# Six modulation buffers in two sets of three, with layer 1's gate tiles in one set and asked for over three groups

## The chip, the core and the metric

The kernel runs on one NeuronCore of one Trainium2 chip. The metric is the device time of one execution in microseconds (us). "PE" is TensorE, "DVE" VectorE, "ACT" ScalarE, "POOL" GpSimd and "SP" SyncE; SP and POOL issue the DMAs, and each issues its own in the order of its list.

## The reference

Two layers of a hybrid encoder over 512 positions of width 2048, in float32. For each layer:

```
mod = silu(c) @ w_ada + b_ada            # 2048 -> 3 x 2048
shift, scale, gate = split(mod)
h = layernorm(x) * (1 + scale) + shift
u_f, z_f, cq, ckv, k_r, z_a = split(h @ w_in)     # 1024 1024 512 256 64 1024
y_f = real(fft over positions and channels of u_f) @ w_fmix * silu(z_f)
q   = rmsnorm(cq) @ w_q_b ;  kv = rmsnorm(ckv) @ w_kv_b ;  rotary on q and k_r
y_a = attention(q, k, v) * silu(z_a)              # 8 heads, not causal
x   = layernorm(alpha * x + gate * (concat(y_f, y_a) @ w_out)) * ln_g + ln_b
```

## The kernel before

**Numbers in two halves.** Each float32 operand is split into a rounded half `hi` and a remainder `lo` (`split`: an ACT cast at L148, a DVE subtraction at L149), and each product is three matmuls (`mm3`, L152 to L154). A weight tile is loaded by SP into one of three raw buffers (pool `wrp`), cast on ACT and subtracted on DVE; the raw buffer is free again after the subtraction.

**Order.** The kernel is written with tile pools. A scheduler lays the program out into one list for each engine and puts in the semaphore waits; each engine then works strictly through its list. A tile of a pool waits for the last reader of the tile that had its buffer before.

**The modulation, L206 to L283.** The product with `w_ada` is not done on PE: tiles of `w_ada` of 128 x 1024 (512 KB) are loaded (`ada_load`), and one DVE instruction a tile multiplies it by a column of silu(c) and adds it to a sum (L246 the first of a block, L248 the rest). A block of 1024 output columns takes 16 tiles; then PE transposes the sum (L261), DVE adds it up (L262). The gate of a layer is two blocks, called block 1 and block 2 below: 32 tiles. Layer 1's gate tiles are loaded by POOL (L213, the `GP` branch); all other modulation tiles by SP. A block's steps stand in a generator; `bg_step(n)` adds n to a credit and takes one step for each whole unit of it, so that n is the number of tiles asked for at one unit of the main program.

**Where the tiles live.** The pool `adp` has six buffers of 4 KB a partition under one tag. They hold, one after another, modulation tiles, the scratch `junk` of a normalisation, transposed x (`xT`), in layer 1 six of the folded Fourier constants (`fc`, L567), and at the end the rows of ln_g and ln_b (`lgb`, L1312, four tiles a layer). While the Fourier stage of layer 1 needs the six constants, no gate tile can be loaded.

**Layer 1's first half.** The in-projection comes in groups of columns: U and ZF[0], then the folded Fourier transform of U (`u_pass`, `fourier_folded`; its last steps L863 to L865 run beside the group ZF[1]), then CQ, CKV and ZA[1]. A group is eight units: one weight tile each, multiplied into four PSUM banks of the pool `psa`, which has four banks. So a group can begin in a bank only when the group before is read out of it: ZF[1] by `unfolded` (ACT copy L880, DVE L881 and L882, ACT silu L883, stored to `szd` by SP), CQ by `latent` (ACT copy L916 of two banks, DVE L917 and L918, then squares on ACT, the power on POOL at L190, the scaling on DVE at L927; PE then transposes the result at L933). Beside CQ, `gates` loads the stored silu values back and multiplies the Fourier rows by them on DVE (L873). Gate tiles are asked for at 0.8 a unit in ZF[0] (`G0`), at 1.6 a unit in CKV and ZA[1] (`G1`), and what is left at 1.4 a unit in the output projection (`CP`). The lines are:

```
banks = fm_group(ada=G0)
...
lq = latent_q(tm_group(CQ, runner(gt)))
...
lkv = latent_kv(tm_group(CKV, runner(lq), G1))
...
unfolded(fm_group(last, G1), 4)
```

**The end.** The output projection takes four groups of eight units; after the first, the gate row of layer 1 must be there: the second block's sum (L261, L262), a store of the gate to DRAM (L270) and its load, spread over the partitions (L1284, L1299), and then the first product with it on DVE (L1257).

Of the kernel before, what the change touches and what calls it, by code (L numbers as in the profile page):

```python
# [9 lines left out]
F32 = mybir.dt.float32  # L10
# [8 lines left out]
P = 128  # L19
S = 512  # L20
# [62 lines left out]
def trunk_kernel(ctx: ExitStack, tc: tile.TileContext, x, c, positions, w_ada, b_ada, w_in, q_norm,  # L83
# [4 lines left out]
    SZ = [1, 2, 3, 4, 6]  # L88
    LEADS = [0.5, 0.6, 0.7, 0.5, 0.5]

    ZP, ZL, AP, CP, G0, G1 = 0.5, 1.0, 1.0, 1.4, 0.8, 1.6

    DL0, DLY = 2, 3

# [15 lines left out]
    wrp = ctx.enter_context(tc.tile_pool(name="wrp", bufs=3))  # L110
    acp = ctx.enter_context(tc.tile_pool(name="acp", bufs=2))
    bp = ctx.enter_context(tc.tile_pool(name="bp", bufs=35))
    adp = ctx.enter_context(tc.tile_pool(name="adp", bufs=6))
    t2p = ctx.enter_context(tc.tile_pool(name="t2p", bufs=9))
    smp = ctx.enter_context(tc.tile_pool(name="smp", bufs=4))
    psa = ctx.enter_context(tc.tile_pool(name="psa", bufs=4, space=PSUM))
# [5 lines left out]
    def nm(s):  # L122
        uid[0] += 1
        return f"{s}{uid[0]}"

    def big(shape, dt=F32R):
        return bp.tile(shape, dt, tag="b", name=nm("b"))
# [3 lines left out]

    def t2(shape, dt=F32):
        return t2p.tile(shape, dt, tag="t2", name=nm("t2"))

    def sm(n, tag):
        return smp.tile([P, n], F32, tag=tag, name=nm(tag), bufs=4 if tag in ('mx', 'ssum') else 2)
# [4 lines left out]
    def pm():  # L141
        return psm.tile([P, 512], F32, tag="pm", name=nm("pm"))

    def f(ap):
        return ap.bitcast(F32)
# [22 lines left out]
    for tb in range(NT):  # L168
        t = [big([P, 1024], F32) for _ in range(2)]
# [17 lines left out]
    def rsqrt_eps(dst, src, n, tag, mul=1.0):  # L187
        t = sm(n, tag + "_v")
        V.tensor_scalar(t, src, mul, EPS, op0=ALU.mult, op1=ALU.add)
        GP.tensor_tensor(dst, t, mhalf[:, :n], op=ALU.pow)  # L190
# [15 lines left out]
    def ada_load(l, r, nr, pieces):  # L206
        w, o = sum(n for _, n in pieces), 0
        if l == 0 and pieces[0][0] < SZ[0] * P:
            t = big([P, nr, w], F32)
        else:  # L210
            t = adp.tile([P, nr, w], F32, tag="ada", name=nm("ada"))
        for c0, n in pieces:
            (GP if l == 1 and c0 >= 32 * P else SP).dma_start(t[:, :, o:o + n],  # L213
                         w_ada[l].rearrange("(p r) c -> p r c", p=P)[:, r:r + nr, c0:c0 + n])
            o += n
        return t
# [104 lines left out]
    def ln_stats(stats, tag):  # L321
        mv = sm(2, tag + "_mv")
        V.bn_aggr(mv, stats)
        rstd = sm(1, tag + "_rstd")
        rsqrt_eps(rstd, mv[:, 1:2], 1, tag)
        return mv, rstd

    def bns():
        return smp.tile([P, 4, 6], F32, tag="bns", name=nm("bns"))
# [7 lines left out]
    def normalise(t, sums=None, note=None):  # L337

        nmr, nmean = sm(1, 'nmr'), sm(1, 'nmean')
        if sums is not None:  # L340
            acc, rstd = sm(2, 'lnacc'), sm(1, 'ln_rstd')
            def junk():
                return adp.tile([P, 1024], F32, tag="ada", name=nm("junk"))

            V.tensor_scalar(nmean, sums[:, 0:1], sums[:, 1:2], -1.0 / D, op0=ALU.add, op1=ALU.mult)
            for j in range(2):
                A.activation(junk(), t[j], AF.Square, bias=nmean, accum_out=acc[:, j:j + 1])
            var = sm(1, 'var')
            V.tensor_scalar(var, acc[:, 0:1], acc[:, 1:2], None, op0=ALU.add)
            rsqrt_eps(rstd, var, 1, 'ln', 1.0 / D)  # L350
        else:
            stats = bns()
            for j in range(4):
                V.bn_stats(stats[:, j], t[j // 2][:, (j % 2) * 512:(j % 2) * 512 + 512])
            mv, rstd = ln_stats(stats, 'ln')
            V.tensor_scalar(nmean, mv[:, 0:1], -1.0, None, op0=ALU.mult)
        V.tensor_tensor(nmr, nmean, rstd, op=ALU.mult)
        if note is not None:
            note.extend([sums[:, 1:2], acc[:, 0:1], rstd])
        for j in range(2):  # L360
            A.activation(t[j], t[j], AF.Identity, scale=rstd, bias=nmr)
# [3 lines left out]
    def transposed(xh, k):  # L365
        ps = pm()
        for tb in range(NT):
            PE.transpose(out=ps[:, tb * P:(tb + 1) * P],
                         in_=xh[tb][k // 8][:, (k % 8) * P:(k % 8) * P + P], identity=ident)
        return ps  # L370
# [79 lines left out]
    def scaled(hi, lo, src, g):  # L450
        A.activation(hi, src, AF.Copy, scale=g)
        V.scalar_tensor_tensor(out=lo, in0=src, scalar=g, in1=f(hi), op0=ALU.mult, op1=ALU.subtract)
# [31 lines left out]
    CQ, CKV, UA, UB = (CQ0, 512), (CKV0, 320), (U0, 512), (U0 + 512, 512)  # L484
# [76 lines left out]
    def folded_constants(l):  # L561


        def keep(shape, dt=F32R):
            n[0] += 1
            if n[0] <= 6:
                return adp.tile(shape, dt, tag="ada", name=nm("fc"))  # L567
            return big(shape, dt)

        n = [0]  # L570
        cw, nq, dt = [[None, None], [None, None]], [], []
        cc = big([P, 2, P], F32)
        GP.dma_start(cc, chan.rearrange("a p c -> p a c"))
        wf = big([P, G, P], F32)
        SP.dma_start(wf, w_fmix[l].rearrange("g m d -> m g d"))
        for hf in range(2):
            for a in range(3):
                lhs = big([P, P], F32)
                if a < 2:
                    for d in range(2):  # L580
                        V.tensor_copy(lhs[:, d * 64:d * 64 + 64], cc[:, a, 0:64])
                else:
                    V.tensor_copy(lhs, cc[:, 0, 64:65].broadcast_to([P, P]))
                ps = pm()
                PE.matmul(ps, lhs, wf[:, hf * 4:hf * 4 + 4].rearrange("p g d -> p (g d)"), start=True, stop=True)
                t = keep([P, 2, 512])
                if a < 2:
                    GP.memset(f(t), 0.0)
                    for d in range(2):
                        rs = slice(d * 64, d * 64 + 64)  # L590
                        o, i = (x.rearrange("p (g e c) -> p g e c", e=2, c=P)[:, :, d] for x in (t[rs, 0], ps[rs]))
                        A.copy(o, i)
                        V.tensor_tensor(t[rs, 1].rearrange("p (g e c) -> p g e c", e=2, c=P)[:, :, d], i, f(o),
                                        op=ALU.subtract)
                    cw[a][hf] = t
                else:
                    for g in range(4):
                        cs, m = slice(g * P, g * P + P), ident[:, 120 + hf * 4 + g:121 + hf * 4 + g]
                        scaled(t[:, 0, cs], t[:, 1, cs], ps[:, cs], m)
                    nq.append(t)  # L600
        for k in range(2):
            t = keep([P, 2, S])
            for a in range(2):
                GP.dma_start(t[:, a], dft[a, k * P:(k + 1) * P, :])
            dt.append(t)
        return cw, nq, dt
# [21 lines left out]
    xT = []  # L628

    def make_xT(k0, k1):  # L630
        for k in range(k0, k1, 2):
            if k0 == 0:
                t = adp.tile([P, 2, S], F32, tag="ada", name=nm("xT"))
            else:
                t = big([P, 2, S], F32)
            for i in range(2):
                A.copy(t[:, i], transposed(xt, k + i))
            xT.append(t)
# [47 lines left out]
    for l in range(DEPTH):  # L686
        sums = {}

        def tm_group(g, work=lambda: None, ada=0):
            banks = [pa() for _ in range(NT)]  # L690
            for k2 in range(8):
                tm_half(banks, st.next(), h, k2 * 2, g[1], k2 == 0, k2 == 7)
                bg_step(ada)
                if k2 < 7:
                    work()
            return banks
# [189 lines left out]
        def runner(gen, n=1):  # L886
            def run():
                for _ in range(n):
                    next(gen, None)
            return run  # L890
# [79 lines left out]
        def latent_q(src):  # L970
            p = latent(src, 512, 512)
            yield
            cq.extend(to_feat(p, k) for k in range(4))
# [146 lines left out]
        if l == 0:  # L1120

            for step, (k0, nk) in enumerate(STEPS):
# [5 lines left out]
                if final:  # L1128
                    cw, dt = fourier_weights(0)
# [50 lines left out]
                lq = latent_q(pq)  # L1180
# [20 lines left out]
        else:  # L1201
# [5 lines left out]
            cw, nq, dt = folded_constants(1)  # L1207
# [2 lines left out]
            unfolded(fm_group(runner(fb, FW)), H + 4)  # L1210
            drain(fb)
            gt = gates()
            lq = latent_q(tm_group(CQ, runner(gt)))
            drain(gt)
            next(lq)
            lkv = latent_kv(tm_group(CKV, runner(lq), G1))
# [14 lines left out]
        for i in range(len(todo) + WL):  # L1231
# [9 lines left out]
            if i < 4:  # L1241
                for k in range(2 * i, 2 * i + 2):
                    t = big([P, 2, S])
# [9 lines left out]
        lgb = {}  # L1253
# [26 lines left out]
        for g in range(4):  # L1280
# [21 lines left out]
            else:  # L1302
# [6 lines left out]
                    tm_half(banks, st.next(), y, k2 * 2, 512, k2 == 0, False)  # L1309
                ws = [st.next() for _ in range(KO, 8)]  # L1310
                for i, src in enumerate((ln_g, ln_b)):
                    lgb[i] = [adp.tile([P, 1024], F32, tag='ada', name=nm('lgb')) for _ in range(2)]  # L1312
                    for j in range(2):
                        SP.dma_start(lgb[i][j], src[l:l + 1, j * 1024:(j + 1) * 1024].broadcast_to([P, 1024]))
                if l == 0:
# [79 lines left out]
```

## Time and profile before

| | us |
|---|---|
| median of 3 runs | 1399.76 (1399.33 to 1401.72) |
| profiled execution | 1403.96 |
| its span | 1402.2 |
| PE busy in the span | 1344.2 (96%) |
| DVE busy | 1013.9 (72%) |
| ACT busy | 582.3 (42%) |
| POOL busy | 55.4 (4%) |

Times inside the kernel are counted from the start of the span, on the profiled execution. Rows of the trace are read so: start, duration, engine, line, operation, output and input tiles by the program's names, and in square brackets the time that the engine sat idle before and what released it. "x3" stands for three instructions one behind the other. A DMA's row on POOL or SP is its issue; its landing is told apart. In layer 1 the group ZF[1] ends and CQ begins near 955, CKV begins near 1003, and the first group of the output projection ends near 1255.

### The profile page before, as it was taken

The page shows a single profiled execution, that of the slowest core. Times are in us where ns is not written, and L with a number is a line of the kernel's source. Part 1 is how long each engine was busy: PE and PEld are TensorE (multiplying, and loading weights), DVE is VectorE, ACT ScalarE, POOL GpSimd, SP SyncE. Part 2 cuts the span into 40 slices and gives each one's busy share as a digit, 9 for nine tenths or more (in the row PEclk, how much of TensorE's full clock was granted, in tenths as well). Part 3 has the DMA queues.
Part 4 walks back from the last instruction along what each step waited for, and adds up shares of the span by engine and source line. Part 5 has one row for each costly group of instructions (what it writes and reads, how often), then busy time and mean ns, then how long its engine had stood idle before and what let it go on. Part 6 is the DMA issues. An engine that isn't in the chain of part 4 may idle for free.

```text
span 1402.2 us, 18752 instructions
## 1 busy us (share of the span) xinstructions
PE 1344.2 (96%) x6979; PEld 1139.3 (81%) x6979; DVE 1013.9 (72%) x1667; ACT 582.3 (42%) x1057; POOL 55.4 (4%) x82
## 2 busy tenths in 40 slices
PE   3899999999999999999998999999999999999996
PEld 3688888787888888878877888887898888888885
DVE  7899999948978986659588658557655576642448
ACT  5713323224537777212248524323234677721210
POOL 1000000000000000000022001011000000000001
PEclk9999999999999999999999999999999999999998
DMA  9988898923763542967446345369544221263323
GB/s 269 290 297 273 276 328 287 361 78 98 224 209 101 181 157 87 326 232 269 138 149 226 107 123 166 105 210 359 170 119 121 74 67 53 83 233 105 91 60 120
DMA packets 134547, 253.26 MB, mean 181 GB/s; under 512 B 19308, under 2 KB 50168, under 8 KB 134456
## 3 DMA queue, kind: packets, MB, share of 16 engines
q1 hardware_dynamic: 127416, 228.73, 50.2%
q0 software_dynamic: 7040, 23.34, 4.8%
q8 instruction: 55, 0.90, 0.3%
q14 instruction: 36, 0.29, 0.1%
HBM read 237.32 MB, written 14.70 MB: 180 GB/s over the span
## 4 chain that ended last, share of the span: by engine, by line
PE 80%; DMA 7%; DVE 7%; issue 3%; ACT 2%; POOL 1%; SPq 0%; DVEq 0%; ACTq 0%; POOLq 0%
PE pa L154 18%; PE pa L152 18%; PE pa L153 18%; PE pm L152 6%; PE pm L153 6%; PE pm L154 6%; DMA ada<-in_w_ada_dram 4%; DMA wr<-in_w_in_dram 3%; PE pm L1091 2%; DVE b L149 2%; PE pa L1071 1%; PE pa L1072 1%; DVE acc L248 1%; ACT b L148 1%; PE pm L261 1%
## 5 line engine op out<-in xcount | busy, mean ns | idle before, releaser
L152 PE MATMUL pa<-b,b 128*128 128x512 f32 (+4 forms) x1408 | 526.9, 376 | 12.3 <-ACT b L148 5.8
L153 PE MATMUL pa<-b,b 128*128 128x512 f32 (+4 forms) x1408 | 525.7, 374 | 1.0 <-DVE b L149 0.9
L154 PE MATMUL pa<-b,b 128*128 128x512 f32 (+4 forms) x1408 | 525.0, 374 | 1.0 <-DVE b L149 1.0
L148 ACT CAST b<-wr 128x1024 fp32r<-128x1024 f32 (+3 forms) x182 | 177.9, 988 | 360.0 <-PE pa L154 181.2
L152 PEld LDWEIGHTS pa<-b,b 128*128 128x128 f32 x1408 | 264.6, 189 | 59.9 <-ACT b L148 9.4
L149 DVE TENSOR_TENSOR b<-wr,b 128x1024 fp32r<-128x1024 f32 (+3 forms) x182 | 205.6, 1140 | 136.3 <-PE pa L153 84.5
L154 PEld LDWEIGHTS pa<-b,b 128*128 128x128 f32 x1408 | 265.5, 189 | 47.3 <-DVE b L149 2.1
L153 PEld LDWEIGHTS pa<-b,b 128*128 128x128 f32 x1408 | 265.7, 189 | 44.7 <-DVE b L149 1.9
L248 DVE SCALAR_TENSOR_TENSOR acc<-ada,cact,acc 128x1024 f32<-128x1024 f32 (+2 forms) x193 | 227.4, 1184 | 22.6 <-DMA ada<-in_w_ada_dram 20.6
L152 PE MATMUL pm<-b,b 128*128 128x512 f32 (+3 forms) x594 | 201.5, 341 | 2.1 <-DVE b L1155 0.9
L153 PE MATMUL pm<-b,b 128*128 128x512 f32 (+3 forms) x594 | 197.0, 333 | 0.0
L154 PE MATMUL pm<-b,b 128*128 128x512 f32 (+3 forms) x594 | 196.7, 332 | 0.0
L152 PEld LDWEIGHTS pm<-b,b 128*128 128x128 f32 x594 | 111.6, 188 | 19.3 <-ACT b L148 2.7
L153 PEld LDWEIGHTS pm<-b,b 128*128 128x128 f32 x594 | 112.1, 189 | 10.5
L154 PEld LDWEIGHTS pm<-b,b 128*128 128x128 f32 x594 | 112.1, 189 | 10.6
L148 ACT CAST b<-pm 128x512 fp32r<-128x512 f32 (+4 forms) x110 | 55.0, 531 | 72.6 <-PE pm L835 17.8
L149 DVE TENSOR_TENSOR b<-pm,b 128x512 fp32r<-128x512 f32 (+4 forms) x110 | 64.2, 610 | 24.1 <-ACT b L148 23.5
L1155 DVE TENSOR_TENSOR b<-b,pm 128x512 f32<-128x512 f32 (+1 forms) x88 | 55.2, 656 | 5.2 <-PE pm L154 5.0
L148 ACT CAST b<-t 128x512 fp32r<-128x512 f32 (+1 forms) x73 | 36.0, 526 | 30.8 <-PE pm L153 9.6
L1074 DVE TENSOR_REDUCE mx<-pa 128x1 f32<-128x512 f32 x64 | 42.9, 684 | 5.2 <-PE pa L1072 4.7
L1079 ACT ACTIVATE t<-t,ssum 128x512 f32<-128x512 f32 x64 | 45.9, 736 | 1.1 <-DVE ssum L1078 1.1
L1077 ACT ACTIVATE t<-pa,mx 128x512 f32<-128x512 f32 x64 | 44.0, 694 | 4.6 <-DVE mx L1074 4.5
(208 smaller groups left out, 1175.3 us busy)
## 6 DMA issues: line engine op xcount, KB each, us to landing
wr<-in_w_in_dram SPq DMA_DIRECT2D x105, 512.0 KB, 4.6
ada<-in_w_ada_dram SPq DMA_DIRECT2D x96, 512.0 KB, 5.4
wr<-in_w_out_dram SPq DMA_DIRECT2D x64, 512.0 KB, 4.2
ada<-in_w_ada_dram SPq DMA_DIRECT2D x96, 256.0 KB, 4.9
ada<-in_w_ada_dram POOLq DMA_DIRECT2D x32, 512.0 KB, 5.5
b<-in_x_dram SPq DMA_DIRECT2D x16, 512.0 KB, 6.8
ada<-in_w_ada_dram SPq DMA_DIRECT2D x32, 192.0 KB, 4.7
wr<-in_w_q_b_dram SPq DMA_DIRECT2D x48, 128.0 KB, 3.0
```

The costliest lines, as they stand in the source:

```text
L148: A.copy(hi, src)
L149: V.tensor_tensor(lo, src, f(hi), op=ALU.subtract)
L152: PE.matmul(o, lh, rh, start=first, stop=False)
L153: PE.matmul(o, lh, rl, start=False, stop=False)
L154: PE.matmul(o, ll, rh, start=False, stop=last)
L248: V.scalar_tensor_tensor(out=a, in0=t[:, r - r0], scalar=cact[:, r:r + 1], in1=a, op0=ALU.mult, op1=ALU.add)
L261: PE.transpose(out=ps[:, o:o + P], in_=acc[:, a, (i + j) * P:(i + j + 1) * P], identity=ident)
L1074: V.reduce_max(mx, ps, axis=AX.X, negate=True)
L1077: A.activation(e, ps, AF.Exp, bias=mx, accum_out=ssum)
L1079: A.activation(e, e, AF.Copy, scale=ssum)
L1091: PE.transpose(out=ps[:, o:o + P], in_=es[q2][:, kb * P:(kb + 1) * P], identity=ident)
L1155: V.tensor_tensor(s_[tb], s_[tb], banks[tb][:, :n], op=ALU.add)
```

## The change

The pool gets two tags, `ada` and `adb`, of three buffers each, through a helper `ad`. It deals tiles out in turn to the two tags, except layer 1's gate tiles (`first`): those always take `ada` and do not count as a turn. The junk, constants, xT and lgb tiles go through `ad` too. The six buffers together are as large as before. `G1` goes from 1.6 to 1.0, and the group CQ is given `G1` too, so that after ZF[0] gate tiles are asked for at one a unit in CQ, CKV and ZA[1]. That makes 6 + 24 tiles, and the last two are asked for in the output projection; before it was 6 + 26. Lines from 141 on stand seven lines further down.

```diff
--- before.py
+++ after.py
@@ -88,7 +88,7 @@
     SZ = [1, 2, 3, 4, 6]
     LEADS = [0.5, 0.6, 0.7, 0.5, 0.5]
 
-    ZP, ZL, AP, CP, G0, G1 = 0.5, 1.0, 1.0, 1.4, 0.8, 1.6
+    ZP, ZL, AP, CP, G0, G1 = 0.5, 1.0, 1.0, 1.4, 0.8, 1.0
 
     DL0, DLY = 2, 3
 
@@ -110,7 +110,7 @@
     wrp = ctx.enter_context(tc.tile_pool(name="wrp", bufs=3))
     acp = ctx.enter_context(tc.tile_pool(name="acp", bufs=2))
     bp = ctx.enter_context(tc.tile_pool(name="bp", bufs=35))
-    adp = ctx.enter_context(tc.tile_pool(name="adp", bufs=6))
+    adp = ctx.enter_context(tc.tile_pool(name="adp", bufs=3))
     t2p = ctx.enter_context(tc.tile_pool(name="t2p", bufs=9))
     smp = ctx.enter_context(tc.tile_pool(name="smp", bufs=4))
     psa = ctx.enter_context(tc.tile_pool(name="psa", bufs=4, space=PSUM))
@@ -131,6 +131,13 @@
 
     def t2(shape, dt=F32):
         return t2p.tile(shape, dt, tag="t2", name=nm("t2"))
+
+    turn = [0]
+
+    def ad(shape, dt, s, first=False):
+
+        turn[0] += 0 if first else 1
+        return adp.tile(shape, dt, tag="ada" if first or turn[0] % 2 else "adb", name=nm(s))
 
     def sm(n, tag):
         return smp.tile([P, n], F32, tag=tag, name=nm(tag), bufs=4 if tag in ('mx', 'ssum') else 2)
@@ -208,7 +215,7 @@
         if l == 0 and pieces[0][0] < SZ[0] * P:
             t = big([P, nr, w], F32)
         else:
-            t = adp.tile([P, nr, w], F32, tag="ada", name=nm("ada"))
+            t = ad([P, nr, w], F32, "ada", l == 1 and pieces[0][0] >= 32 * P)
         for c0, n in pieces:
             (GP if l == 1 and c0 >= 32 * P else SP).dma_start(t[:, :, o:o + n],
                          w_ada[l].rearrange("(p r) c -> p r c", p=P)[:, r:r + nr, c0:c0 + n])
@@ -340,7 +347,7 @@
         if sums is not None:
             acc, rstd = sm(2, 'lnacc'), sm(1, 'ln_rstd')
             def junk():
-                return adp.tile([P, 1024], F32, tag="ada", name=nm("junk"))
+                return ad([P, 1024], F32, "junk")
 
             V.tensor_scalar(nmean, sums[:, 0:1], sums[:, 1:2], -1.0 / D, op0=ALU.add, op1=ALU.mult)
             for j in range(2):
@@ -564,7 +571,7 @@
         def keep(shape, dt=F32R):
             n[0] += 1
             if n[0] <= 6:
-                return adp.tile(shape, dt, tag="ada", name=nm("fc"))
+                return ad(shape, dt, "fc")
             return big(shape, dt)
 
         n = [0]
@@ -630,7 +637,7 @@
     def make_xT(k0, k1):
         for k in range(k0, k1, 2):
             if k0 == 0:
-                t = adp.tile([P, 2, S], F32, tag="ada", name=nm("xT"))
+                t = ad([P, 2, S], F32, "xT")
             else:
                 t = big([P, 2, S], F32)
             for i in range(2):
@@ -1210,7 +1217,7 @@
             unfolded(fm_group(runner(fb, FW)), H + 4)
             drain(fb)
             gt = gates()
-            lq = latent_q(tm_group(CQ, runner(gt)))
+            lq = latent_q(tm_group(CQ, runner(gt), G1))
             drain(gt)
             next(lq)
             lkv = latent_kv(tm_group(CKV, runner(lq), G1))
@@ -1309,7 +1316,7 @@
                     tm_half(banks, st.next(), y, k2 * 2, 512, k2 == 0, False)
                 ws = [st.next() for _ in range(KO, 8)]
                 for i, src in enumerate((ln_g, ln_b)):
-                    lgb[i] = [adp.tile([P, 1024], F32, tag='ada', name=nm('lgb')) for _ in range(2)]
+                    lgb[i] = [ad([P, 1024], F32, 'lgb') for _ in range(2)]
                     for j in range(2):
                         SP.dma_start(lgb[i][j], src[l:l + 1, j * 1024:(j + 1) * 1024].broadcast_to([P, 1024]))
                 if l == 0:
```

What the scheduler makes of it: until the end of the Fourier stage the lists hold the same rows in the same order, but for one memset on POOL. Three places change. In the rows, a name with a number is one tile; tiles `ada` are gate tiles, `acc` the block's sum.

First place: DVE at the end of the Fourier stage, beside the group ZF[1]. Before:

```order
L149 TENSOR_TENSOR b_8640<-pm_8652,b_8640 128x255
L248 SCALAR_TENSOR_TENSOR acc_7577<-ada_9225,cact,acc_7577 128x1024
L248 SCALAR_TENSOR_TENSOR acc_7577<-ada_9228,cact,acc_7577 128x1024
L248 SCALAR_TENSOR_TENSOR acc_7577<-ada_9293,cact,acc_7577 128x1024
L863 TENSOR_TENSOR b_8691<-t_8703,pm_8693 128x255
L864 TENSOR_TENSOR b_8691<-t_8703,pm_8693 128x255
L865 COPY b_8691<-t_8703 128x2
L248 SCALAR_TENSOR_TENSOR acc_7577<-ada_9326,cact,acc_7577 128x1024
```

and changed:

```order
L156 TENSOR_TENSOR b_8640<-pm_8652,b_8640 128x255
L255 SCALAR_TENSOR_TENSOR acc_7577<-ada_8930,cact,acc_7577 128x1024
L870 TENSOR_TENSOR b_8691<-t_8703,pm_8693 128x255
L871 TENSOR_TENSOR b_8691<-t_8703,pm_8693 128x255
L872 COPY b_8691<-t_8703 128x2
L255 SCALAR_TENSOR_TENSOR acc_7577<-ada_8966,cact,acc_7577 128x1024
L870 TENSOR_TENSOR b_8691<-t_8719,pm_8709 128x255
L871 TENSOR_TENSOR b_8691<-t_8719,pm_8709 128x255
L872 COPY b_8691<-t_8719 128x2
L156 TENSOR_TENSOR b_8725<-wr_8598,b_8724 128x1024
```

Three gate products in a row, of tiles in three buffers, stood there; now each stands apart from the next, because all go through one buffer (two of the three buffers of `ada` hold constants until the stage's last step). Up to the end of the stage there are 11 gate products on DVE before and 5 now.

Second place: DVE at the end of CQ, where the products of the gate end and the read-out of CQ begins (`pa` is CQ's bank, `t` the copy of another). Before:

```order
L248 SCALAR_TENSOR_TENSOR acc_9476<-ada_9965,cact,acc_9476 128x1024
L248 SCALAR_TENSOR_TENSOR acc_9476<-ada_10032,cact,acc_9476 128x1024
L248 SCALAR_TENSOR_TENSOR acc_9476<-ada_10098,cact,acc_9476 128x1024
L248 SCALAR_TENSOR_TENSOR acc_9476<-ada_10101,cact,acc_9476 128x1024
L248 SCALAR_TENSOR_TENSOR acc_9476<-ada_10174,cact,acc_9476 128x1024
L248 SCALAR_TENSOR_TENSOR acc_9476<-ada_10177,cact,acc_9476 128x1024
L917 TENSOR_TENSOR b_9164<-pa_8896,t_9166 128x512
L918 TENSOR_TENSOR b_9164<-pa_8896,t_9166 128x512
```

and changed:

```order
L255 SCALAR_TENSOR_TENSOR acc_9347<-ada_9893,cact,acc_9347 128x1024
L255 SCALAR_TENSOR_TENSOR acc_9347<-ada_9965,cact,acc_9347 128x1024
L255 SCALAR_TENSOR_TENSOR acc_9347<-ada_10032,cact,acc_9347 128x1024
L255 SCALAR_TENSOR_TENSOR acc_9347<-ada_10098,cact,acc_9347 128x1024
L255 SCALAR_TENSOR_TENSOR acc_9347<-ada_10171,cact,acc_9347 128x1024
L255 SCALAR_TENSOR_TENSOR acc_9347<-ada_11616,cact,acc_9347 128x1024
L255 SCALAR_TENSOR_TENSOR acc_9347<-ada_11651,cact,acc_9347 128x1024
L924 TENSOR_TENSOR b_9188<-pa_8896,t_9190 128x512
L925 TENSOR_TENSOR b_9188<-pa_8896,t_9190 128x512
```

In both lists all 26 gate products that come after ZF[0] stand ahead of the read-out of CQ, those asked for in the output projection (ada_11616, ada_11651) among them. Before, the last 10 stand in a row; now the last 15 do, and their tiles go through three buffers instead of six. POOL's power for the read-out (L190) stands behind all the gate loads in both lists.

Third place: ACT at the start of CQ, the copies that clear the banks of ZF[1] (`pa`) and the casts of CQ's weights (`wr`). Before:

```order
L148 CAST b_8933<-wr_8842 128x1024
L880 COPY t_8868<-pa_8396 128x512
L880 COPY t_8875<-pa_8397 128x512
L883 ACTIVATE t_8869<-t_8869 128x512
L148 CAST b_8966<-wr_8904 128x1024
L883 ACTIVATE t_8876<-t_8876 128x512
L880 COPY t_8882<-pa_8398 128x512
L148 CAST b_8999<-wr_8937 128x1024
L880 COPY t_8889<-pa_8399 128x512
```

and changed:

```order
L155 CAST b_8936<-wr_8842 128x1024
L887 COPY t_8868<-pa_8396 128x512
L155 CAST b_8972<-wr_8904 128x1024
L887 COPY t_8875<-pa_8397 128x512
L890 ACTIVATE t_8869<-t_8869 128x512
L155 CAST b_9008<-wr_8940 128x1024
L887 COPY t_8882<-pa_8398 128x512
L890 ACTIVATE t_8876<-t_8876 128x512
L155 CAST b_9044<-wr_8976 128x1024
L890 ACTIVATE t_8883<-t_8883 128x512
L887 COPY t_8889<-pa_8399 128x512
```

Each copy but the first stands behind one more cast: the fourth copy (pa_8399) stood behind the casts of CQ's fourth, fifth and sixth weight, and now stands behind that of the seventh (wr_8976) as well.

Two smaller moves: the PE transposes of block 1 stand some hundred rows earlier, those of block 2 stand 48 rows further down in the first group of the output projection, and two of the four lgb loads stand far earlier on SP. The other two wait for the last gate tiles.

## Rows read from the trace of the kernel before

**Rows 1.** The page, busy time of each engine over the span

```profile
PE 1344.2 (96%) x6979; PEld 1139.3 (81%) x6979; DVE 1013.9 (72%) x1667; ACT 582.3 (42%) x1057; POOL 55.4 (4%) x82
```

**Rows 2.** Busy time by stretch: PE, PEld, DVE, ACT, POOL, PEclk, DMA share, GB/s

```profile
925.00:955.00 30.00, 30.00 (x161) 25.62 (x160) 24.38 (x35) 8.85 (x15) 8.97 (x17) 1.00 0.86 287
955.00:965.00 10.00, 6.90 (x28) 4.73 (x27) 7.26 (x12) 5.83 (x10) 0.53 (x1) 1.00 1.03 403
965.00:1003.00 38.00, 38.00 (x169) 31.46 (x168) 27.26 (x28) 4.68 (x6) 4.23 (x8) 1.00 0.87 306
```

**Rows 3.** Waits, 925 to 1010: total us, times, longest

```profile
PE pa L152 <- ACT t L880: 3.1, 2, 1.6
...
PE pm L933 <- DVE b L927: 0.9, 1, 0.9
```

**Rows 4.** Timeline of ACT at the start of CQ: start, us

```profile
961.84 1.04 ACT L148 CAST b<-wr 128x1024 fp32r<-128x1024 f32 x1 [1.67 <-DMA wr<-in_w_in_dram]
962.79 0.58 ACT L880 COPY t<-pa 128x512 f32<-128x512 f32 x1
```

**Rows 5.** Weight loads issued at 929.2, 951.0 and 958.2: last number us to landing

```profile
wr<-in_w_in_dram SPq DMA_DIRECT2D x1, 512.0 KB, 4.1
wr<-in_w_in_dram SPq DMA_DIRECT2D x1, 512.0 KB, 10.8
wr<-in_w_in_dram SPq DMA_DIRECT2D x1, 512.0 KB, 7.4
```

**Rows 6.** Timeline of DVE, the gate products and what follows

```profile
929.34 3.96 DVE L248 SCALAR_TENSOR_TENSOR acc<-ada,cact,acc 128x1024 f32<-128x1024 f32 x3
...
982.06 0.69 DVE L873 TENSOR_TENSOR b<-b,t 128x512 f32<-128x512 f32 x1
982.66 13.17 DVE L248 SCALAR_TENSOR_TENSOR acc<-ada,cact,acc 128x1024 f32<-128x1024 f32 x10
1002.51 0.69 DVE L917 TENSOR_TENSOR b<-pa,t 128x512 f32<-128x512 f32 x1 [6.68 <-ACT t L916]
...
1008.25 1.68 DVE L927 TENSOR_SCALAR b<-b,rrstd 128x512 f32<-128x512 f32 x4 [1.17 <-POOL rrstd L190]
```

**Rows 7.** Timeline of POOL, issues of gate loads

```profile
925.18 1.58 POOL L213 DMA_DIRECT2D ada<-in_w_ada_dram  x3 [45.12 <-PE pm L154]
930.92 0.53 POOL L213 DMA_DIRECT2D ada<-in_w_ada_dram  x1 [4.17 <-DVE acc L248]
...
984.24 0.53 POOL L213 DMA_DIRECT2D ada<-in_w_ada_dram  x1 [2.61 <-DVE acc L248]
```

**Rows 8.** Landing of the gate loads issued at 984.24, 985.56 and 986.88

```profile
DMA to landing us min/median/max: 3.8/3.8/3.8
DMA to landing us min/median/max: 4.8/4.8/4.8
DMA to landing us min/median/max: 5.4/5.4/5.4
```

**Rows 9.** Busy time by stretch, within the gate run (columns as rows 2)

```profile
990.00:996.00 6.00, 6.00 (x29) 4.95 (x28) 5.68 (x5) 0.00 (x0) 0.00 (x0) 1.00 0.95 310
```

**Rows 10.** Timeline of POOL and DVE, the early gate tiles of block 1

```profile
751.83 2.25 POOL L213 DMA_DIRECT2D ada<-in_w_ada_dram  x4 [0.32 <-issue]
...
792.16 2.60 DVE L248 SCALAR_TENSOR_TENSOR acc<-ada,cact,acc 128x1024 f32<-128x1024 f32 x2
...
798.68 1.28 DVE L248 SCALAR_TENSOR_TENSOR acc<-ada,cact,acc 128x1024 f32<-128x1024 f32 x1
```

**Rows 11.** Timeline of PE, wait for a column sum of block 1

```profile
1046.38 0.51 PE L1022 MATMUL pm<-identr,t 128*128 128x128 f32 x4 [0.26 <-DVE red L262]
```

**Rows 12.** Output projection: transposes of block 2, gate row load (issued at 1238.5), DVE product

```profile
1231.47 1.03 PE L261 MATMUL pm<-ident,acc 128*128 128x128 f32 x8
...
t<-gated SPq DMA_DIRECT2D x1, 256.0 KB, 7.2
...
1255.94 0.70 DVE L1257 TENSOR_TENSOR pa<-pa,t 128x512 f32<-128x512 f32 x1 [0.30 <-PE pa L154]
```

## The prediction

> **What bounds the kernel now.** I read the page first. PE is busy 96% of its span [rows 1], so a change that gives it no other work moves the time only where PE is made to wait, or stops waiting. The change touches layer 1's gate tiles, so the second view is the busy time by stretch around them [rows 2]: PE is full from 925 to 955 and from 965 to 1003, and in the ten microseconds between, where CQ begins, it works 6.90 us. The DMA share there is 1.03, and 0.86 on either side: the transfers are near their limit wherever gate tiles are loaded. The list of waits [rows 3] puts PE's gap down to 3.1 us of waiting for the copies of ZF[1]'s banks (L880). ACT's timeline shows why: the fourth copy stands behind a cast that waited for its weight's DMA [rows 4], and that weight took 10.8 us to land, against 4.1 for one loaded when fewer were under way [rows 5].
>
> The second place is the end of CQ. On DVE the last ten gate products run in one piece, 13.17 us, 1.32 each, and end at 995.8 [rows 6]. L917 starts at 1002.51 after 6.68 us of waiting for CQ's own result, so the gate work has 6.7 us of slack here. Behind L917 there is none: squares, power and scaling follow each other, and PE already waited 0.9 us for the scaling L927 [rows 3, 6]. Whatever makes L917 late makes PE as late.
>
> **The change, part by part.** No engine gets more or less work, and PE's list differs in order alone. What changes is how many gate loads can be under way, and what stands ahead of what.
>
> *One buffer during the Fourier stage.* Before, three buffers come free at 925, three loads are issued, and a product that starts at 929.34 lets the next load go at 930.92 [rows 6, 7]: 1.58 us from a product's start to the next issue. With one buffer, a tile takes this 1.58 plus its landing, 3.8 to 5.4 [rows 8], so 5.4 to 7.0 a tile. In the 27 us up to CQ that makes four to five tiles, and the list has five there, where it had eleven. That costs PE nothing here: the DVE products stand behind work that PE needs, but each waits for a tile loaded one round earlier. Six products are put off to CQ.
>
> *The start of CQ.* The fourth copy now stands behind the cast of the seventh weight. Before, that weight was issued at 958.2 [rows 5]. Landing in 4.1 (fewer gate loads are in the way), cast in 1.04 and copied in 0.58 [rows 4], its bank is clear at 963.9, against 962.79 + 0.58 = 963.4 before; landing in 7.4 [rows 5], at 967.2. From the other side, all the 3.1 us could go. So this step lies between 3.1 less and 3.8 more. I take no shift, since the shorter landing gives + 0.5 and the weight's buffer is freed a little sooner by the new order.
>
> *The run of gate products at the end of CQ.* This is the term of the sum. Fifteen products stand in a row now, behind the last L873, which ends at 982.7, and the tiles go through three buffers: three products, then a wait for the next three. A round is 1.58 + 3.8 = 5.38 us with the landing of a load that had none close ahead of it [rows 8]. The transfers allow it: three tiles are 1.57 MB, at the 310 GB/s that were moved here [rows 9] 5.07 us. The fifth round begins at 982.66 + 4 × 5.38 = 1004.2, and its third product ends 2 × 1.32 + 1.28 later, at 1008.1. L917 began at 1002.51: **5.6 us late**, and PE with it. With the landings of the next two loads in a chain, 4.8 and 5.4, the round is 6.38 or 6.98 and the end 1012.1 or 1014.5: 9.6 or 12.0 late. I take 3.8, because with three loads in a round the wait is for the first. Nothing on PE takes this up later: after CQ it waits for hardly anything that is not behind the same chain.
>
> The Trainium skill ("DMA: Bandwidth & Descriptors", section on the anatomy of one DMA on the gpsimd path) gives such a load about 2.0 us plus its bytes at 436 GB/s; for 512 KB that is an estimate of 3.2 us. The trace is longer, 3.8 at the least. By the page the round would be 4.8 and the run would end at 1005.8, and the sum would be + 3.0 instead of + 5.3.
>
> *The rest.* The early gate tiles at 751.83 are six; now three go early and three after the first products, from 792.16 on [rows 10]. Landing 3.8 to 5.4 later, the first of them is there before its product at 798.68: nothing. Block 1's sum is added up earlier, which can take away PE's 0.26 us of waiting for it [rows 11]: − 0.3. Block 2's transposes come 48 matmuls later, 48 × 38.00 / 169 = 10.8 us [rows 2], at 1242.3 instead of 1231.47. The gate row's load was issued 7.0 us after the transposes and landed in 7.2 [rows 12]: now at 1256.5, and the product that needs it started at 1255.94. PE comes back to that bank after three other banks of six matmuls, 4.1 us, so 0.6 us is covered: nothing, though a microsecond more would begin to cost. The two late lgb loads wait on SP for the last gate tile; the next weight behind them waits for DVE work that comes after L917 anyway: nothing.
>
> **Sum:** 5.6 − 0.3 = + 5.3 us. The profiled execution took 1403.96, so this would be 1409.3 in it; it lies 4.2 above the median of the runs, and against that median, 1399.76, the forecast is **1405.1 us**.
>
> **The rivals.**
>
> *PE gains at CQ's start, and the run keeps up.* With six buffers, gate and weight loads met at 1.03 of the DMA share [rows 2]; with fewer gate loads the weights land in 4.1 instead of 10.8, the 3.1 us go, the whole of CQ comes 3.1 earlier and the run starts at 979.6. If its tiles are all there, its 15 × 1.32 = 19.8 us end at 999.4, just when L917 would be due; then the time is 1399.76 − 3.1 − 0.3 = 1396.4. The point that decides: the round must be at most 1.32 × 3 = 4.0 us. Against it: with three buffers that wants a landing of 2.4, and the shortest here is 3.8 [rows 8]. A scheduler's list can also prove different on the chip in where the last L873 ends. Chance 0.12. The Trainium skill (same page, section on SWDGE, HWDGE and iDMA) says that each DMA engine goes round-robin between the queues that the two ways of issuing feed, so that fewer POOL loads leave SP's weights more turns; the landings of 4.1 and 10.8 agree with it.
>
> *Half of that.* CQ starts 3.1 earlier, the run starts at 979.6 and its rounds take what the transfer takes, 5.07 [rows 9]: it ends at 979.6 + 20.3 + 3.9 = 1003.8, 1.3 late, − 0.3: 1400.8, no difference that can be told. For it: weights and gate tiles compete visibly. Against it: the gates' own loads and weights on SP pace the L873 products too. Chance 0.16.
>
> *Worse.* The loads of a round pile up as the three of rows 8 do, the round is 6.38, L917 is 9.6 late: + 9.3, 1409.1; a fourth copy at 967.2 moves the start of the run by as much as 3.8 and gives the same. Chance 0.12.
>
> *The change doesn't do what it says.* "One tile a unit over three groups" is the pace of asking. On DVE all 26 products still stand ahead of CQ's read-out, so the slower pace doesn't spread them over CKV and ZA[1], and the price above follows from this. Had they been spread, there would be no run, and the first rival's price would hold; its chance is in that rival.
>
> **How the numbers follow.** The forecast has 0.60. About 2.8 us (0.2%) is what a measurement of this kernel can tell from no change. The forecast and the worse case are slower by more than that, but for a small part where the start of CQ gains as well: slower 0.70; same 0.17, with the second rival; faster 0.13, with the first. The range reaches from 1398.3, which leaves out most of the first rival, to 1409.5, which holds the worse case at its first landing and leaves out its second. The forecast's own range is 1403.9, with rounds of 5.07, to 1407.1, with a landing midway between 3.8 and 4.8.
>
> **What the profile would show.** Right: the waits on DVE at the last gate products name the gate DMA; L924 (L917 before) starts behind them with no wait for ACT, some 5 us later against CQ's end; PE's wait for L934 (L927) grows from 0.9 to about 6 us; POOL issues one gate load every 5 to 7 us from 925 to 952. Wrong: DVE waits for CQ's copy before L924, as now, or the gate run starts before 978; or PE's waits at the start of CQ exceed 7 us, which would put the loss there instead.

## Result and profile after

The changed kernel took 1414.34 us (median of 4 runs, 1412.96 to 1414.75), the kernel before 1400.74 beside it: 1.009 times as long, 95% interval [1.0075, 1.0104]. Slower, as forecast, but by 13.6 us where 5.3 stood in the sum, and above the range that was given (1398.3 to 1409.5).

The page of the changed kernel, its span and the busy time of each engine:

```profile
span 1411.2 us, 18759 instructions
...
PE 1347.7 (95%) x6979; PEld 1142.5 (81%) x6979; DVE 1014.1 (72%) x1667; ACT 582.3 (41%) x1057; POOL 56.0 (4%) x82
```

The span is 9.0 us longer for the same work. The two profiled executions differ before the change begins to act, so I count from one point of the program, the first gate load that follows the U pass (at 925.18 before, [rows 7]; at 921.73 now). This common point stands for time 0 wherever a time is said to be counted from it. From there to the end of the span it was 477.0 us before and is 489.5 now: 12.5 us, all of it behind this point. Busy time by stretch, in the columns of [rows 2], with one stretch more:

```profile
925.00:955.00 30.00, 28.18 (x145) 23.36 (x143) 16.91 (x27) 7.47 (x12) 3.69 (x7) 1.00 0.61 199
955.00:965.00 10.00, 6.65 (x17) 4.70 (x18) 7.22 (x11) 7.51 (x11) 0.53 (x1) 0.71 0.92 314
965.00:1003.00 38.00, 38.00 (x167) 31.37 (x166) 26.25 (x27) 2.05 (x4) 8.33 (x15) 0.99 0.89 298
1003.00:1050.00 47.00, 39.37 (x252) 38.02 (x251) 26.22 (x57) 15.08 (x35) 3.37 (x5) 0.93 0.45 137
```

PE still loses about three microseconds where CQ begins, at a lower clock now (0.71 for that stretch), and 7.6 us more between 1003 and 1050. PE's waits after 900 name them, in total, times and longest:

```profile
PE pa L159 <- DVE b L925: 7.6, 1, 7.6
PE pa L159 <- ACT t L887: 3.8, 2, 3.3
```

L925 is what L918 was: DVE's read-out of CQ, for which PE waits before CKV's third bank. That is one step earlier than I had named: the wait for the scaling (L934), which was to grow to about 6 us, is gone. POOL's issues of gate loads in the Fourier stage come one by one, 5.5 us apart, where they came in threes before [rows 7]:

```profile
921.73 0.53 POOL L220 DMA_DIRECT2D ada<-in_w_ada_dram  x1 [45.84 <-PE pm L161]
929.48 0.53 POOL L220 DMA_DIRECT2D ada<-in_w_ada_dram  x1 [7.22 <-DVE acc L255]
934.97 0.53 POOL L220 DMA_DIRECT2D ada<-in_w_ada_dram  x1 [4.96 <-DVE acc L255]
940.47 0.53 POOL L220 DMA_DIRECT2D ada<-in_w_ada_dram  x1 [4.97 <-DVE acc L255]
```

On DVE, the run of fifteen gate products and the read-out behind it (before: [rows 6], ten in one piece and then a wait for ACT):

```profile
981.46 1.28 DVE L255 SCALAR_TENSOR_TENSOR acc<-ada,cact,acc 128x1024 f32<-128x1024 f32 x1
984.19 2.60 DVE L255 SCALAR_TENSOR_TENSOR acc<-ada,cact,acc 128x1024 f32<-128x1024 f32 x2 [1.45 <-DMA ada<-in_w_ada_dram]
987.55 1.28 DVE L255 SCALAR_TENSOR_TENSOR acc<-ada,cact,acc 128x1024 f32<-128x1024 f32 x1 [0.76 <-DMA ada<-in_w_ada_dram]
...
1010.95 1.28 DVE L255 SCALAR_TENSOR_TENSOR acc<-ada,cact,acc 128x1024 f32<-128x1024 f32 x1 [0.84 <-DMA ada<-in_w_ada_dram]
1012.15 0.68 DVE L924 TENSOR_TENSOR b<-pa,t 128x512 f32<-128x512 f32 x1
```

The read-out L924 begins at 1012.15 with no wait for ACT: the last gate product, which waited for its load, released it. That is 90.4 us after the common point, and it was 77.3: **13.1 us late, where I had 5.6**. The chain of work that ended last says the same for this stretch, in start and length; between 979 and 1012 it goes from gate load to gate product and back, and PE is not in it:

```profile
979.11 4.98 DMA ada<-in_w_ada_dram
984.19 1.29 DVE acc L255
985.51 1.30 DVE acc L255
...
987.09 4.86 DMA ada<-in_w_ada_dram
...
993.62 4.82 DMA ada<-in_w_ada_dram
...
1000.12 4.47 DMA ada<-in_w_ada_dram
...
1006.27 4.59 DMA ada<-in_w_ada_dram
...
1012.15 0.68 DVE b L924
```

### The profile page after: what moved, and what is told of

Its sections match the earlier page's. It is cut to its first block, busy times and chain, and to the rows that moved or that the text cites. A ratio compares the mean times of both kernels' runs of the same rounds, so it can differ in the third digit from the quotient of the medians.

```text
span 1411.2 us, 18759 instructions
## 1 busy us (share of the span) xinstructions
PE 1347.7 (95%) x6979; PEld 1142.5 (81%) x6979; DVE 1014.1 (72%) x1667; ACT 582.3 (41%) x1057; POOL 56.0 (4%) x82
```

## Experiments

**My theory after the result:** the whole loss is the lateness of the gate products that stand ahead of CQ's read-out, because they go through three buffers. **Rivals:** the new pace; the start of CQ, where PE waits and its clock falls; the dealing of the other tiles to two tags. In the table, times are counted from the common point in each kernel's profiled execution; the ratio is that of the runs to those of the kernel before, with its interval.

| kernel | CQ read-out starts | its transposes on PE | end of span | ratio to before |
|---|---|---|---|---|
| before | 77.3 | 83.6 | 477.0 | |
| changed | 90.4 | 96.4 | 489.5 | 1.0090 [1.0075, 1.0104] |
| pace | 79.0 | 85.2 | 478.6 | 1.0008 [0.9992, 1.0024] |
| sets | 89.2 | 95.7 | 488.9 | 1.0095 [1.0074, 1.0116] |
| after_copies | 86.0 | 92.4 | 485.5 | 1.0076 [1.0058, 1.0094] |
| after_held | 78.8 | 85.1 | 485.5 | 1.0072 [1.0055, 1.0089] |
| four | 80.0 | 86.2 | 479.6 | 1.0001 [0.9985, 1.0018] |
| before_copies | 73.4 | 79.7 | 473.2 | 0.9967 [0.9949, 0.9984] |
| after_spread | 72.8 | 79.1 | 475.5 | 1.0000 [0.9985, 1.0016] |
| six_spread | 73.4 | 79.7 | 473.8 | 0.9967 [0.9951, 0.9983] |

**pace: the pace without the sets.** On the kernel before:

```diff
-    ZP, ZL, AP, CP, G0, G1 = 0.5, 1.0, 1.0, 1.4, 0.8, 1.6
+    ZP, ZL, AP, CP, G0, G1 = 0.5, 1.0, 1.0, 1.4, 0.8, 1.0
-            lq = latent_q(tm_group(CQ, runner(gt)))
+            lq = latent_q(tm_group(CQ, runner(gt), G1))
```

> The kernel before (six buffers, one tag) with only the pace of the change: G1 at 1.0, asked for in CQ, CKV and ZA[1]. Buffers theory: DVE's list up to the read-out of CQ is that of before, ten products at its end, so the time is that of before, 1400.7 within 2 us, and PE's waits at the start of CQ stay about 3.1 us. Pace rival: what costs time is asking for gate tiles beside CQ; then this run loses most of the 13 us and lies near 1412.

No difference from before that the runs can tell: 1401.5 us. PE's wait for the copies at the start of CQ was longer in this execution than before's 3.1 us:

```profile
PE pa L152 <- ACT t L880: 4.6, 3, 2.9
```

**sets: the sets without the pace.** The two edits above, undone in the changed kernel.

> The changed kernel with the old pace (G1 at 1.6, none asked for in CQ), so the two sets of three alone. Buffers theory: fifteen products in a row through three buffers as in the changed kernel, so the time is that of the change, 1413 to 1415. Pace rival: near before, 1401.

All of the loss: 1413.4 us. PE waits for the read-out and for the copies; of the second line 3.6 us, in three pieces, stand at the start of CQ, the rest in an earlier group:

```profile
PE pa L159 <- DVE b L925: 9.3, 1, 9.3
PE pa L159 <- ACT t L887: 4.5, 4, 2.4
```

The pace falls as a cause; the two sets alone make the change's time. The run says one thing more. Here CKV begins 79.3 us after the common point and in the changed kernel at 82.1, and the read-out and the end are within about one microsecond of each other all the same. How late PE finishes CQ does not matter: it waits for the read-out anyway, 9.3 us here and 7.6 there.

**after_copies: the start of CQ put right.** On the changed kernel, `copied` being the last copy of `unfolded` (L887):

```diff
             for k2 in range(8):
-                tm_half(banks, st.next(), h, k2 * 2, g[1], k2 == 0, k2 == 7)
+                with tc.issue_after(behind) if behind and k2 else nullcontext():
+                    w = st.next()
+                tm_half(banks, w, h, k2 * 2, g[1], k2 == 0, k2 == 7)
...
-            lq = latent_q(tm_group(CQ, runner(gt), G1))
+            lq = latent_q(tm_group(CQ, runner(gt), G1, behind=copied[0]))
```

> The changed kernel; the casts of CQ's weights from the fourth on are put behind ACT's four copies that clear the banks of ZF[1], by order alone. Theory: the waits of PE at the start of CQ (3.3 and 0.5 us) and the drop of its clock behind them go, some 4 us; but the run of fifteen products still ends about where it did unless it starts earlier too. If it starts 4 us earlier with CQ: 1410. If its end is set by its own loads: 1413 to 1414, and the wait before CKV's third bank grows from 7.6 to about 11 us. Rival, that the start of CQ alone is the loss: 1402.

1410.7 us, the time of the first case; the longer wait is that of the second. PE has hardly a wait left at the start of CQ, and waits at its end instead:

```profile
PE pa L159 <- DVE b L930: 12.0, 1, 12.0
```

On DVE the run begins 2.5 us earlier than in the changed kernel, counted from the common point, and not 4, but its products still wait for their loads and end with no wait of the read-out behind them:

```profile
976.47 2.60 DVE L255 SCALAR_TENSOR_TENSOR acc<-ada,cact,acc 128x1024 f32<-128x1024 f32 x2
...
1004.09 1.28 DVE L255 SCALAR_TENSOR_TENSOR acc<-ada,cact,acc 128x1024 f32<-128x1024 f32 x1 [0.29 <-DMA ada<-in_w_ada_dram]
1005.29 0.68 DVE L929 TENSOR_TENSOR b<-pa,t 128x512 f32<-128x512 f32 x1
```

So the start of CQ costs only as far as it makes the run begin late. PE came to CKV 73.4 us after the common point, 8.7 earlier than in the changed kernel, and at the end 4.0 of that are left.

**after_held: the run taken away.** On the changed kernel, `tail` being DVE's last instruction of CQ's read-out, set after `next(lq)`:

```diff
-                stop[0] = next(bg, False)
+                if tail[0] is None:
+                    stop[0] = next(bg, False)
+                else:
+                    with tc.issue_after(tail[0]):
+                        stop[0] = next(bg, False)
```

> The changed kernel; the gate products asked for from CKV on are put behind the scaling of CQ's read-out on DVE, by order alone, so that no run of them stands ahead of the read-out. Theory: PE's wait of 7.6 us before CKV's third bank and the slow matmuls behind it go, about 8 us: 1406, with the 3.3 us wait at the start of CQ left. Rival, that the start of CQ is the loss: 1413. Rival, that the products only move their cost to where the second read-out stands: 1410 or more, with a new wait of PE between 1010 and 1050.

1410.0 us. The read-out came 11.6 us earlier than in the changed kernel, and only 4 us were gained. The last rival was the right one. PE's waits after 900:

```profile
PE pa L159 <- ACT t L893: 4.5, 4, 1.8
PE pa L159 <- DVE b L931: 3.5, 1, 3.5
```

L931 is the second read-out, CKV's; on DVE two gate products stand ahead of it that waited 3.4 us for a load:

```profile
1038.35 2.61 DVE L255 SCALAR_TENSOR_TENSOR acc<-ada,cact,acc 128x1024 f32<-128x1024 f32 x2 [3.40 <-DMA ada<-in_w_ada_dram]
1040.87 0.48 DVE L930 TENSOR_TENSOR b<-pa,t 128x320 f32<-128x320 f32 x1
```

The products moved, and with them the hold-up. In this execution's stretch from 1040 to 1050 PE was busy 6.62 us of 10 at a clock of 0.80, where its full stretches show 0.95.

**four: sets of four and two.** The gate tiles have four buffers, and the other tiles are dealt out four and two:

```diff
-        return adp.tile(shape, dt, tag="ada" if first or turn[0] % 2 else "adb", name=nm(s))
+        gate = first or turn[0] % 6 in (1, 2, 3, 5)
+        return adp.tile(shape, dt, tag="ada" if gate else "adb", name=nm(s), bufs=4 if gate else 2)
```

> The changed kernel with sets of four and two buffers in place of three and three; the gate tiles have four. DVE's list then has eleven products ahead of CQ's read-out, and ACT's copies stand behind fewer casts. Buffers theory with the round measured in the changed kernel (1.58 us from a product to the next issue and 4.6 to land, 6.2 us for as many products as there are buffers): two rounds and three products, 16.4 us, from a start at about 58 us after the end of the U pass, so an end at 75 where the read-out begins at 77: no loss, 1400 to 1403. Rival, that the cost goes with each buffer taken from the gate tiles: a third to two thirds of the loss, 1405 to 1409. Rival, that it is the turn of the other tiles through the two sets (constants, ln rows) that costs: 1410 or more.

No loss that the runs can tell: 1401.4 us. Eleven products stand in the run; it ends just ahead of the read-out, which waits for ACT again, 0.73 us:

```profile
983.73 3.92 DVE L256 SCALAR_TENSOR_TENSOR acc<-ada,cact,acc 128x1024 f32<-128x1024 f32 x3
...
998.45 2.65 DVE L256 SCALAR_TENSOR_TENSOR acc<-ada,cact,acc 128x1024 f32<-128x1024 f32 x2 [0.23 <-DMA ada<-in_w_ada_dram]
1001.83 0.69 DVE L925 TENSOR_TENSOR b<-pa,t 128x512 f32<-128x512 f32 x1 [0.73 <-ACT t L924]
```

In this execution the read-out comes 2.7 us later than before, and the end of the span 2.6; PE waited 3.7 us in one piece for the copies at the start of CQ. The cost does not go with each buffer taken away. It begins where the run ends behind CQ, and dealing tiles to two tags costs nothing that these runs show.

**before_copies: the same order on the kernel before.** The edit of after_copies, on six buffers at the old pace.

> The kernel before with the casts of CQ's weights from the fourth on put behind ACT's four copies, by order alone. Theory: PE's 3.1 us of waits at the start of CQ go, the run of ten products has its slack of 6.7 us, of which 3 are used up: 3 us faster, 1398. Rival, that the weights are late then: no gain, 1401, with waits of PE for casts in CQ.

Faster than both kernels: medians of 1395.7 us against 1402.2 beside it; the ratio, 0.9967, makes it some 4.6 us, and the end of the span in the table 3.8. ACT's timeline shows the last copies ahead of the cast:

```profile
952.17 0.57 ACT L884 COPY t<-pa 128x512 f32<-128x512 f32 x1
952.64 1.05 ACT L148 CAST b<-wr 128x1024 fp32r<-128x1024 f32 x1
```

and DVE's the run of ten and the read-out, whose wait for ACT has gone down from 6.68 us [rows 6] to 0.80:

```profile
980.23 13.16 DVE L248 SCALAR_TENSOR_TENSOR acc<-ada,cact,acc 128x1024 f32<-128x1024 f32 x10
994.20 0.69 DVE L922 TENSOR_TENSOR b<-pa,t 128x512 f32<-128x512 f32 x1 [0.80 <-ACT t L921]
```

The slack that I read in [rows 6] was there; this order uses nearly all of it, 3.9 us by the earlier read-out and 1.9 because the run itself begins later, 59.4 us after the common point against 57.5.

**after_spread and six_spread: all three orders put right.** Copies ahead of casts; products asked for in CKV behind CQ's read-out; those asked for later behind CKV's, by a second line after `next(lkv)`:

```diff
             next(lkv)
+            tail[0] = [i for i in nc.cur_bb.bb.instructions if i.engine == mybir.EngineType.DVE][-1]
```

six_spread has the same with one pool of six and the new pace.

> The changed kernel with three things put in order and nothing else: the copies ahead of the casts at the start of CQ, the gate products asked for in CKV behind the scaling of CQ's read-out, those asked for in ZA[1] and later behind the scaling of the second read-out. Theory: the three-buffer set costs only through the three places where it holds up PE; with all three clear the two sets cost nothing: 1398 to 1401. Rival, that three buffers are too few for 26 tiles wherever they stand: 1405 or more, with a new wait of PE after 1030 or in the output projection.

> The same three orders and the pace of one tile a unit, in one pool of six buffers. Theory: PE's waits at the start of CQ go and no other comes: 1397 to 1399, and within 2 us of the same orders on two sets of three. Rival, that six loads at a time crowd out SP's weights: 1401 to 1404, with PE waiting for casts in CKV or ZA[1].

With the products spread, two sets of three take 1400.9 us, the time of the kernel before, and six buffers 1396.9 us. PE's longest wait after 900 in after_spread:

```profile
PE pm L1040 <- DVE t L465: 2.6, 1, 2.6
```

and the two longest in six_spread:

```profile
PE pm L944 <- DVE b L938: 0.9, 1, 0.9
PE pa L152 <- ACT b L148: 0.6, 1, 0.6
```

So the 13 us are gone on three buffers once nothing urgent stands behind the products. Not all of that is due to spreading them, since the order of the copies alone gives the kernel before about 4 us (before_copies). Like for like, two sets of three are still 4.0 us slower than six buffers: the expectations had put them within 2 us of each other, and that was missed. The wait that the two executions differ by is PE's 2.6 us for the rotary part of the queries (L1040), which DVE brought late in after_spread; counted from the common point their ends are 1.7 us apart, and where the rest of the 4 us comes from I did not follow up.

## Why the prediction was wrong

Right: which engine, which place and which mechanism. The gate products ran through one buffer in the Fourier stage at one load every 5.5 us, five of them; fifteen stood ahead of the read-out; L924 had no wait for ACT; PE stood still for the read-out, though at CKV's third bank and not at the transposes. That the pace is not what stands on DVE is shown by pace and sets.

Wrong: **the term of the run, 5.6 us, measured 13.1**. It had three parts, of which two failed.

1. *The round, 5.38 us.* I built it on a landing of 3.8, the shortest of [rows 8], "because with three loads in a round the wait is for the first". The loads issued from 981 to 1006 in the changed kernel landed so:

```profile
DMA to landing us min/median/max: 3.9/4.5/6.0
```

With 4.5 the round is 6.1. Measured from the rows of DVE, the first, fourth, seventh, tenth and thirteenth product begin at 981.46, 987.55, 993.4, 1001.07 and 1007.10: four rounds of 6.4 on average (5.8 to 7.7). That is my "worse" rival, whose 6.38 came from the second landing of [rows 8]. The 310 GB/s of [rows 9] with which I defended the short round were POOL's and SP's loads together; from 996 to 1003 the gate loads alone moved 255 GB/s, 2.06 us for a tile and 6.2 for three. That was not the most that could be moved: in four, with four buffers and no load of SP's beside them, it was 300 from 985 to 996, at a median landing of 5.0. What set the round was issue and landing in each buffer, not a limit of 255. The fifteen products took 30.7 us, not 25.4: **5.3 of the missing 7.5 us**.

The reason that I gave for the shortest landing is what failed. DVE did not wait for the first load of three and then find the other two there; it waited before eleven of the fifteen products, and each buffer was a chain of its own. The one that ended last is in the chain of work above. Its first product, the third of the run, began 1.4 us later than in my sum, because the load of the product ahead of it, issued at 979.11, took 4.98. Four rounds of 1.58 plus landings of 4.86, 4.82, 4.47 and 4.59 followed, 3.9 us more than four of 5.38.

2. *The start of the run, 982.7, taken as unshifted.* It began 59.7 us after the common point, and 57.5 before: **2.2 us**. The step is "I take no shift". ACT's timeline shows what was late:

```profile
956.23 1.04 ACT L155 CAST b<-wr 128x1024 fp32r<-128x1024 f32 x1 [3.52 <-DMA wr<-in_w_in_dram]
957.18 0.58 ACT L887 COPY t<-pa 128x512 f32<-128x512 f32 x1
...
960.55 1.04 ACT L155 CAST b<-wr 128x1024 fp32r<-128x1024 f32 x1
...
962.14 0.57 ACT L887 COPY t<-pa 128x512 f32<-128x512 f32 x1
```

Each copy waits for the cast ahead of it and that for a weight. The fourth copy comes 40.4 us after the common point, and 37.6 before [rows 4]; the silu rows that go through DRAM from there come back later, and the products L880 ahead of the run with them (DVE waited 3.6 us for these rows in three pieces, and 1.9 in two before). I had put the copy's shift at + 0.5, by a weight that lands in 4.1. The weight that holds up the second copy landed in 8.3, the next in 9.6: with fewer gate loads beside them (four issued from 945 to 955, where there were seven) the weights came in hardly sooner than the 10.8 of [rows 5]. The gain that the first rival drew from the Trainium skill's rule of turns between the two kinds of queue ("DMA: Bandwidth & Descriptors", section on SWDGE, HWDGE and iDMA) did not show here. The Trainium skill's 3.2 us for a gate load (same page, section on the anatomy of one DMA on the gpsimd path), an estimate of the prediction, lies further from the 4.5 measured than the 3.8 of the trace.

3. *The list* of fifteen was right.

The "worse" rival had both halves, a round of 6.38 and a later start, but priced them as one or the other; they came together, and the time lies above its 1409.1.

PE lost 12.8 us at the transposes behind the read-out, and 12.5 at the end. The rest of the sum held: the wait for block 1's column sum [rows 11] went, 0.3 us, and the output projection shows no new wait of PE. One step that I put at nothing did cost: PE waited 1.3 us in the Fourier stage for a DVE subtraction behind a gate product whose load was late. I take it that it did not count in the end, since the run was later still; no run takes it away by itself.

The first rival was wrong with two sets, but its price was real elsewhere: before_copies takes away the 3.1 us of waits by putting the copies ahead of the casts, which has nothing to do with how many gate loads are under way.

## What to carry to other kernels

Before fewer buffers are given to a stream of loads, multiply out the longest row of its consumers that the scheduler has put ahead of something urgent: products in a row, over buffers, times issue plus landing, with the median landing and not the shortest. Here that is 15 / 3 × 6.1 = 30.4 us, and 30.7 were measured. In these runs fewer buffers cost little (nothing that can be told in four, 4 us in after_spread against six_spread) as long as that row ended ahead of the urgent work, and 13 us where it ended behind it. Where an engine's list holds cheap urgent work behind work that waits for a DMA, an order edge between the two can be worth more than a change of buffers or pace: here it gave 0.3% on the untouched pools, where the new pace gave nothing that can be told.

## What was not expected of the hardware

PE's granted clock fell after its waits. At the start of CQ it had waited 3.29 us, worked for less than 2 us, and then ran at half its clock, 0.50 between 960 and 965, which is 1.2 of 2.4 GHz: matmuls follow each other at 0.42 us (the last two rows) instead of 0.23.

```profile
957.81 0.50 PE L159 MATMUL pa<-b,b 128*128 128x512 f32 x1 [3.29 <-ACT t L887]
958.14 0.39 PE L160 MATMUL pa<-b,b 128*128 128x512 f32 x1
...
960.77 0.63 PE L160 MATMUL pa<-b,b 128*128 128x512 f32 x1
961.19 0.63 PE L161 MATMUL pa<-b,b 128*128 128x512 f32 x1
```

Before, 3.1 us of waiting in two pieces of 1.55 left it at 1.00 [rows 2]. The length of the wait alone does not tell: in pace a wait of 2.89 us left it at 1.00 from 955 to 960, and in sets the matmuls behind one of 2.37 us followed each other at 0.42 (0.75 from 955 to 960). In the changed kernel thirteen matmuls ran slow at the start of CQ, some 2.8 us in all; there the run of gate products, which ended later still, hid it. The clock fell again behind the 7.6 us before CKV's third bank (0.53 from 1010 to 1015).

With nothing but POOL's gate loads under way less was moved than in a mixed stretch: 244 to 255 GB/s between 990 and 1003, where POOL and SP together moved 310 before. A single load was little sooner there, 4.5 us at the median against 5.1 for those issued from 976 to 989 before. With a fourth load at a time (four, 985 to 996) it was 300.
